# A two-layer hybrid backbone on one core: layer 0's FFN input product by one level of Strassen's algorithm

## The chip, the cores and the metric

The kernel runs on one core of a Trainium2 chip. The time is the device time of one execution in microseconds (us); lower is better. The time before is the median of three runs. The engines are named as in the profile: PE is TensorE (matrix products, with PEld its weight loads), DVE is VectorE, ACT is ScalarE, POOL is GpSimd, SP is the engine whose queue issues the DMAs.

## The reference

Two layers are computed over 512 latent tokens and 256 context tokens with 1024 channels. Each layer normalises its input, multiplies by one combined input projection, runs four mixers (attention, Fourier, convolution, pooling), multiplies their concatenation by `w_out`, adds the residual, and then runs a gated FFN. Layer 1 computes only the latent tokens after its keys and values. What the change touches is the FFN:

```python
def swiglu(x, w_in, w_out):              # D_MODEL 1024, D_FF 2816
    a, g = jnp.split(x @ w_in, 2, axis=-1)
    return (jax.nn.silu(a) * g) @ w_out

    x = x + gate1 * mix
    xn = rms_norm(x, g2) * (1 + scale2) + shift2
    return x + gate2 * swiglu(xn, w_fi, w_fo)
```

In layer 0 this is done for both streams, 768 tokens with the same weights; in layer 1 for the 512 latent tokens.

## The kernel before

Activations lie with channels on the partitions: eight tiles of 128 channels, `x[0]` to `x[7]`, 768 tokens wide. To keep fp32 accuracy with TensorE's rounded fp32 format, each operand is cut into a rounded part (an ACT cast, "h") and the rest (a difference, "l"), and `mm3` makes three matmuls of each product: h x h, h x l, l x h.

A FIFO list `queue` (lines 229 to 260) holds every weight load in the order of use; `need` (line 274) issues up to two entries ahead. A load is one DMA of 512 KB from SP's queue into a raw tile, an ACT cast and a difference of 1024 columns (`split`, line 180) on VectorE or, in the mixers, on POOL (`lo_eng`). All these tiles come from the pool `wp` of 15 buffers, three per load.

The FFN (line 1083) goes over 22 chunks of 128 hidden columns. For a chunk, `ag` (line 1133) makes two products, a and g, each over eight channel tiles: for the 512 latent tokens 48 matmuls of 512 columns, for the 256 context tokens 48 of 256. `glu` (line 1089) then makes silu(a) x g and cuts it into h and l. A step takes two chunks; `out_step` (line 1145) multiplies the two chunks of the step before with `w_ffn_out`: for each of eight output tiles six matmuls of 512 and six of 256 columns, and one VectorE instruction per stream that adds the result to x. In layer 0 a filler makes 1/8 of layer 1's modulation in each step. In the last step the order is: both products of chunk 20, the latent product of chunk 21, the output product of step 9, the latent half of step 10 with the norm of the next layer, and only then the context product of chunk 21 and the context half of step 10. The first step is `first_step` (line 1103), with the channel tiles as the outer loop, since they become ready one after the other: the second norm's `rstd` and `apply` run on VectorE and ACT beside the last `w_out` products (`proj`).

PSUM has eight banks: two tiles `pb` of two banks, two `pt` and two `pf`. The hidden tiles hh and hl rotate over four tags (g, c, u, b). The mixers take their activations from `alp` (16 tiles of 512 columns, latent) and `acp` (16 of 256, context), and have tiles of their own for u, the attention result and the transposed queries.

The framework gives a tile its buffer and each engine its order of instructions when the program is built: it plays the program through a timing model, and at each engine starts the ready instruction that stands earliest in the program. So latent, context and output matmuls are interleaved. On the chip each engine runs its queue in that fixed order.

Of the kernel before, what the change touches and what calls it, by code (L numbers as in the profile page):

```python
# [44 lines left out]
Pace = namedtuple("Pace", "cols taps0 step0 taps side fill share side_n")  # L45
PACE = (Pace(12, 6, 3, 2, 4, 3.0, 0.7, 10), Pace(8, 10, 2, 2, 2, 3.0, 0.3, 8))
# [3 lines left out]
def kernel(ctx: ExitStack, tc: tile.TileContext, xT, ctxT, vec, cst, dft,  # L50
# [16 lines left out]
    tags.update(g0=(816, 1), g1=(816, 1), c0=(784, 1), c1=(784, 1), a0=(768, 1), a1=(784, 1), u0=(768, 1), u1=(768, 1),  # L67
                b0=(792, 1), b1=(792, 1), pr=(784, 3), t=(792, 4), qt=(512, 3))
# [5 lines left out]
    def AL(name, dt=F32R):  # L74
        return alp.tile([P, NL], dt, tag="al", name=name)
# [73 lines left out]
    rtab = [cp.tile([P, 4, HD], F32, name=f"rt{i}") for i in range(4)]  # L149
# [28 lines left out]
    lo_eng = [dve]  # L178
# [49 lines left out]

    for l in range(DEPTH):
        wi = w_in[l]  # L230
        for kp in range(4):
            queue.append((("qkv", l, kp), lambda wi=wi, kp=kp: load(rows(wi[256 * kp:256 * kp + 256, 0:OFF_F]), "wq")))
        for b in range(2):
            for h in range(2):
                queue.append((("c", l, b, h), lambda wi=wi, b=b, h=h: load_conv(wi, b, h)))
        for b in range(2):
            queue.append((("p", l, b), lambda wi=wi, b=b: load(rows(wi[:, OFF_P + 128 * b:OFF_P + 128 * b + 128]), "wi")))
        for h in range(2):
            queue.append((("u", l, h), lambda wi=wi, h=h: load(rows(wi[512 * h:512 * h + 512, OFF_F:OFF_C]), "wi")))
        queue.append((("sm", l), lambda l=l: load_small(l)))  # L240
        queue.append((("dft", l), lambda l=l: load_dft(l)))
        queue.append((("fold", l), lambda l=l: load_fold(l)))
        for m in range(KD):
            queue.append((("o", l, m), lambda l=l, m=m: load(rows(w_out[l][:, 128 * m:128 * m + 128]), "wo")))

        def fa(c, l=l):
            queue.append((("fa", l, c), lambda: load(rows(w_ffn_in[l][:, 128 * c:128 * c + 128]), "fa")))
            queue.append((("fg", l, c), lambda: load(rows(w_ffn_in[l][:, DFF + 128 * c:DFF + 128 * c + 128]), "fg")))

        def fo(c, l=l):  # L250
            queue.append((("fo", l, c), lambda: load(rows(w_ffn_out[l][128 * c:128 * c + 128, :]), "fo")))

        for s in range(NF // 2):
            fa(2 * s)
            if s:
                fo(2 * s - 2)
                fo(2 * s - 1)
            fa(2 * s + 1)
        fo(NF - 2)
        fo(NF - 1)  # L260
# [104 lines left out]
    class Norm:  # L365


        def __init__(self, nm, direct=KD - 2):
            self.direct = direct
            if direct:  # L370
                self.acc = [U(f"acc{nm}{i}", f"a{i}") for i in range(2)]
# [59 lines left out]

    class Acts:


        def __init__(self, nm, ctx_=True):
            self.lt = [[AL(f"{nm}{i}{k}") for k in range(KD)] for i in "hl"]
            self.ct = [[acp.tile([P, NC], F32R, tag="ac", name=f"{nm}c{i}{k}") for k in range(KD)] for i in "hl"] if ctx_ else None

        def at(self, i, k, sl):
            if sl.start >= NL:  # L440
                return self.ct[i][k][:, sl.start - NL:sl.stop - NL]
            return self.lt[i][k][:, sl]
# [6 lines left out]


    def rope_tables(l):
        for i, (off, f) in enumerate(((V_QG, 1.0), (V_KG, HD ** -0.5))):
# [42 lines left out]
    def mix_phase(l, norm, A, filler):  # L495
# [32 lines left out]
        ksb = U("ksb", "a0")  # L528
# [146 lines left out]
        usb = [U(f"us{j}", f"u{j}") for j in range(2)]  # L675
# [86 lines left out]
        def fourier_prep():  # L762
            B, B2 = AL("fb", F32), AL("fd", F32)
# [7 lines left out]
            if not last:  # L771
                C = AL("fc", F32)
# [6 lines left out]
        def fourier():  # L779
# [11 lines left out]
            for b in range(2):  # L791
# [5 lines left out]
                gh, gl = (U(f"g{b}{i}", "ub"[b] + str(i), F32R)[:, 0:768] for i in range(2))  # L797
# [9 lines left out]
            for o in range(2):  # L807
# [5 lines left out]
                q, t = AL("fqs", F32), AL("ft", F32)  # L813
# [13 lines left out]
            for b in range(2):  # L827
# [3 lines left out]
                gh, gl = (U(f"g{b}{i}", "ub"[b] + str(i), F32R)[:, 0:512] for i in range(2))  # L831
# [20 lines left out]
        at = [U(f"at{j}", ("a0", "x5")[j]) for j in range(2)]  # L852
# [4 lines left out]
        def make_qT(i):  # L857
            j, o = qpos(i)
            st = U("qst", "qt", F32R)
# [7 lines left out]
            qTs[i] = U("qT", "qt", F32R)  # L867
            act.copy(out=qTs[i][:, 0:512], in_=ps)
# [167 lines left out]
        def add(m, sl, s, ps):  # L1036
            dve.scalar_tensor_tensor(out=x[m][:, sl], in0=ps, scalar=modT[l][:, 16 + m, s:s + 1], in1=x[m][:, sl],
                                     op0=ALU.mult, op1=ALU.add)
            n2.square(m, sl)

        def proj(m, w, sl, s, ps):
            ps = ps[:, 0:sl.stop - sl.start]
            part(m, w, sl, ps)
            add(m, sl, s, ps)
        first, second = ((HA, 0), (HB, 0)) if last else ((LAT, 0), (CTX, 1))
# [5 lines left out]
        pb1 = None if last else PB("wo2")  # L1051
        for m in range(4):
            w = held[m] = need(("o", l, m))
            part(m, w, LAT, pts[m], order[:6])
        pcs = [] if last else [pb1[:, 0:256], pb1[:, 512:768]]
        for m, pc in enumerate(pcs):
            part(m, held[m], CTX, pc, order[:6])
        for m in range(4):
            part(m, held[m], LAT, pts[m], order[6:])
            add(m, LAT, 0, pts[m])  # L1060
            if m < len(pcs):
                part(m, held[m], CTX, pcs[m], order[6:])
                add(m, CTX, 1, pcs[m])
            elif not last:
                proj(m, held[m], CTX, 1, PF("wo"))
            held.pop(m)
        ahead[0] = 2
        for m in range(4, KD):
            w = held[m] = need(("o", l, m))
            proj(m, w, *first, PA("wo"))  # L1070
        n2.rstd(first[0])
        A = Acts("xf", not last)
        for m in range(2, KD + 2, 2):
            for k in (m - 2, m - 1):
                n2.apply(l, 1, k, *first, A)
            proj(m // 2 + 3, held.pop(m // 2 + 3), *second, PA("wo"))
        n2.rstd(second[0])
# [5 lines left out]
    def ffn(l, norm, first, second, A, filler):  # L1083
# [15 lines left out]
        def newh(c):  # L1099
            tg = ("g", "c", "u", "b")[c % 4]  # L1100
            h[c] = (U("hh", tg + "0", F32R), U("hl", tg + "1", F32R))

        def first_step():
# [3 lines left out]
            for sl, s in (first, second):  # L1107
                n = sl.stop - sl.start
                wide = n == 512
                if wide or last and sl is first[0]:  # L1110
# [52 lines left out]
        first_step()  # L1163
        for s in range(1, ns):
# [136 lines left out]
```

## Time and profile before

| | |
|---|---|
| median of 3 runs | 1496.5 us (1494.83 to 1497.45) |
| profiled execution | 1496.42 us |
| its span, first to last instruction | 1494.6 us |
| instructions | 20629 |
| busy: TensorE, weight loads | 1450.2 us (97%), 1207.1 us (81%) |
| busy: VectorE, ScalarE, POOL | 778.7 us (52%), 541.4 us (36%), 198.3 us (13%) |
| mean granted TensorE clock | 0.993 |

Busy time is the sum of instructions' durations, overlaps counted once. Matmuls overlap, so a full share says that one was always in flight, and not at which rate they came; the rate is read from starts. The granted clock is a share of 2.4 GHz; 0.50 is its lower level of 1.2 GHz.

### The profile page before, as it was taken

To read this page: it belongs to the slowest core of one execution; us is meant where nothing else is said; L and a number is where in the kernel's file an instruction comes from. 1 tells how busy PE (TensorE), PEld (TensorE's weight loads), DVE (VectorE), ACT (ScalarE), POOL (GpSimd) and SP (SyncE) were. 2 spreads that over 40 slices of the span, in tenths; PEclk is the share of its full clock that TensorE was granted. 3 is DMA by queue.
4 is the path that set the end of the run, shared out by engine and by line. 5 is a ranking of instruction groups with operands and counts; after the bars stand their busy time and mean duration, and the time that the engine had idled before them with its cause. 6 is when DMAs were issued, how large, how long until landed. Compare 5 with 4: busy or idle time off the path is not lost.

```text
span 1494.6 us, 20629 instructions
## 1 busy us (share of the span) xinstructions
PE 1450.2 (97%) x8538; PEld 1207.1 (81%) x8538; DVE 778.7 (52%) x1204; ACT 541.4 (36%) x876; POOL 198.3 (13%) x161
## 2 busy tenths in 40 slices
PE   7999889999999999999999999899999999999998
PEld 4687777888888888888888887677789888888887
DVE  3569478354543444344334357587646545444444
ACT  4457656433222112211211234657545322222220
POOL 2435411500000000000000024341330000000000
PEclk9999999999999999999999999999999999999999
DMA  8624444212123213222331231446632323333331
GB/s 281 188 85 149 148 154 131 85 57 83 60 71 99 85 57 99 85 63 79 107 91 43 71 99 57 134 137 198 198 99 87 108 88 99 94 104 90 95 99 57
DMA packets 192926, 157.35 MB, mean 105 GB/s; under 512 B 6464, under 2 KB 179520, under 8 KB 192832
## 3 DMA queue, kind: packets, MB, share of 16 engines
q1 hardware_dynamic: 192544, 155.34, 33.9%
q8 instruction: 67, 1.10, 0.3%
q10 hardware_dynamic: 288, 0.69, 0.1%
q14 instruction: 27, 0.22, 0.0%
HBM read 151.81 MB, written 4.19 MB: 104 GB/s over the span
## 4 chain that ended last, share of the span: by engine, by line
PE 85%; DVE 7%; ACT 3%; DMA 2%; POOL 1%; issue 1%; SPq 0%; DVEq 0%; ACTq 0%
PE ag L161 33%; PE fo L161 21%; PE agc L161 7%; PE wo L161 6%; PE mod L161 3%; PE qkv L161 2%; DVE run L565 2%; PE u L161 2%; PE ssq L161 2%; PE cv L161 1%; PE S L161 1%; PE pv L161 1%; DMA wi<-in_w_in_dram 1%; PE PT L167 1%; PE pp L161 1%
## 5 line engine op out<-in xcount | busy, mean ns | idle before, releaser
L1152 DVE SCALAR_TENSOR_TENSOR x<-fo,mod,x 128x512 f32<-128x512 f32 (+1 forms) x264 | 172.3, 660 | 139.8 <-PE fo L161 139.4
L161 PE MATMUL fo<-hh,foh 128*128 128x512 f32 (+1 forms) x528 | 188.7, 358 | 1.9 <-DVE ht L1095 1.9
L161 PE MATMUL fo<-hh,fol 128*128 128x512 f32 (+1 forms) x528 | 188.8, 357 | 0.0
L161 PE MATMUL fo<-hl,foh 128*128 128x512 f32 (+1 forms) x528 | 188.6, 357 | 0.0
L182 ACT CAST foh<-fo 128x1024 fp32r<-128x1024 f32 x44 | 46.1, 1048 | 275.3 <-PE fo L161 218.5
L161 PE MATMUL ag<-xfh,fah 128*128 128x512 f32 (+1 forms) x368 | 140.4, 386 | 1.2 <-ACT xfh L428 1.2
L161 PE MATMUL ag<-xfl,fah 128*128 128x512 f32 (+1 forms) x368 | 140.7, 382 | 0.6 <-DVE xfl L429 0.5
L161 PE MATMUL ag<-xfh,fal 128*128 128x512 f32 (+1 forms) x368 | 140.5, 382 | 0.0
L161 PE MATMUL ag<-xfh,fgh 128*128 128x512 f32 (+1 forms) x368 | 140.0, 381 | 0.0
L161 PE MATMUL ag<-xfh,fgl 128*128 128x512 f32 (+1 forms) x368 | 140.0, 381 | 0.0
L161 PE MATMUL ag<-xfl,fgh 128*128 128x512 f32 (+1 forms) x368 | 139.8, 380 | 0.0
L161 PEld LDWEIGHTS fo<-hh,foh 128*128 128x128 f32 x528 | 99.6, 189 | 18.9 <-DVE ht L1095 2.1
L161 PEld LDWEIGHTS fo<-hl,foh 128*128 128x128 f32 x528 | 100.0, 189 | 16.7
L161 PEld LDWEIGHTS fo<-hh,fol 128*128 128x128 f32 x528 | 100.1, 190 | 15.7
L105 DVE TENSOR_TENSOR fal<-fa,fah 128x1024 fp32r<-128x1024 f32 x42 | 51.7, 1231 | 101.4 <-ACT fah L182 101.4
L105 DVE TENSOR_TENSOR fgl<-fg,fgh 128x1024 fp32r<-128x1024 f32 x42 | 51.4, 1224 | 97.3 <-ACT fgh L182 86.4
L565 DVE SCALAR_TENSOR_TENSOR run<-glu,vt,run 128x512 f32<-128x512 f32 (+1 forms) x98 | 86.9, 887 | 1.1
L182 ACT CAST fah<-fa 128x1024 fp32r<-128x1024 f32 x44 | 46.2, 1049 | 100.8 <-DMA fa<-in_w_ffn_in_dram 90.2
L182 ACT CAST fgh<-fg 128x1024 fp32r<-128x1024 f32 x44 | 46.1, 1048 | 97.9 <-DMA fg<-in_w_ffn_in_dram 89.1
L161 PEld LDWEIGHTS ag<-xfh,fah 128*128 128x128 f32 x368 | 69.0, 188 | 15.0 <-ACT xfh L428 1.4
L161 PEld LDWEIGHTS ag<-xfl,fah 128*128 128x128 f32 x368 | 69.2, 188 | 14.2 <-DVE xfl L429 1.4
L161 PEld LDWEIGHTS ag<-xfh,fgl 128*128 128x128 f32 x368 | 69.2, 188 | 13.1
(335 smaller groups left out, 3140.8 us busy)
## 6 DMA issues: line engine op xcount, KB each, us to landing
wm<-in_w_mod_dram SPq DMA_DIRECT2D x64, 512.0 KB, 4.6
fa<-in_w_ffn_in_dram SPq DMA_DIRECT2D x44, 512.0 KB, 3.9
fg<-in_w_ffn_in_dram SPq DMA_DIRECT2D x44, 512.0 KB, 3.9
fo<-in_w_ffn_out_dram SPq DMA_DIRECT2D x44, 512.0 KB, 3.3
wm<-in_w_mod_dram SPq DMA_DIRECT2D x40, 256.0 KB, 5.7
wo<-in_w_out_dram SPq DMA_DIRECT2D x16, 512.0 KB, 5.3
wm<-in_w_mod_dram SPq DMA_DIRECT2D x16, 384.0 KB, 5.6
x<-in_xT_dram SPq DMA_DIRECT2D x16, 256.0 KB, 4.1
```

Source lines behind the costliest of these rows:

```text
L105: eng.tensor_tensor(out=out, in0=full, in1=b32(hi), op=ALU.subtract)
L161: i = last_pe[0] = pe.matmul(*a, **kw)
L167: i = last_pe[0] = pe.transpose(*a)
L182: act.copy(out=hi[:, :n], in_=raw[:, :n])
L565: yield dve.scalar_tensor_tensor(out=cacc[b][:, :cwid] if j == CONVW - 1 else run, in0=glu[b][:, j:j + cwid], scalar=tap(b, j), in1=cacc[b ...
L1152: dve.scalar_tensor_tensor(out=x[m][:, sl], in0=ps[:, :n], scalar=modT[l][:, 40 + m, st:st + 1], in1=x[m][:, sl], op0=ALU.mult, op1=ALU.add)
```

## The change

Layer 0 (`FAST = (True, False)`) keeps the ordinary product for chunks 0 and 1. For chunks 2 to 21 the product of the 256 x 1024 weight block (a on top of g) with the 1024 x 768 activations is split in two along each of its three dimensions: output rows a and g, channels 0 to 511 and 512 to 1023, tokens 0 to 383 and 384 to 767. Winograd's form of Strassen's algorithm makes it with 7 products of half size, four sums of weights and four of activations, and seven additions of results. Each product has four channel tiles and three matmuls of 384 columns. The sums are made in fp32, and then cut into h and l: weights seven times 512 columns per chunk (all on VectorE and ACT), activations once for the layer. `w_out` of layer 0 is made in two halves of 384 tokens too, the second with one instruction more where the streams meet. In the last step chunk 21's product is made before the output products, and both halves of the latent stream come before the context stream.

To make room, tiles of 768 columns in one pool of 28 (`alp`) hold the operands, the mixers' activations of both streams, u, the first attention result, the queries, the rotary tables and one norm sum; Fourier scratch tiles move into `wp`, which goes from 15 to 14 buffers; and hidden tiles rotate over three tags. The scratch for DMA descriptors is set to 1024. Both layers' mixers use the shared pool.

```diff
-    alp = ctx.enter_context(tc.tile_pool(name="alp", bufs=16))
-    acp = ctx.enter_context(tc.tile_pool(name="acp", bufs=16))
-    wp = ctx.enter_context(tc.tile_pool(name="wp", bufs=15))
+    alp = ctx.enter_context(tc.tile_pool(name="alp", bufs=28))
+    wp = ctx.enter_context(tc.tile_pool(name="wp", bufs=14))
...
+    def load_ff(l, c):
+        raws = []
+        for o in (0, DFF):
+            raw = RAW("ff")
+            nc.sync.dma_start(out=raw.rearrange("p (a b) -> p a b", b=P), in_=rows(w_ffn_in[l][:, o + P * c:o + P * c + P]))
+            raws.append(raw)
+        a1, a2, g1, g2 = (r[:, 512 * i:512 * i + 512] for r in raws for i in range(2))
+        ops = {}
+        def cut(nm, full):
+            w = ops[nm] = W("f" + nm)
+            hi, lo = w[:, 0:512], w[:, 512:1024]
+            act.copy(out=hi, in_=full)
+            sub_lo(lo_eng[0], lo, full, hi)
+        def comb(out, in0, in1, op):
+            sum_eng[0].tensor_tensor(out=out, in0=in0, in1=in1, op=op)
+        cut("a11", a1)
+        cut("a12", a2)
+        cut("a22", g2)
+        comb(g2, g1, g2, ALU.add)
+        comb(g1, a1, g1, ALU.subtract)
+        comb(a1, g2, a1, ALU.subtract)
+        comb(a2, a2, a1, ALU.subtract)
+        for nm, full in (("s2", a1), ("s3", g1), ("s1", g2), ("s4", a2)):
+            cut(nm, full)
+        return ops
...
+    class Operands:
...
+        def cut(self, nm, k, full, eng=None):
+            act.copy(out=self.h(nm, k), in_=full)
+            sub_lo(eng or dve, self.l(nm, k), full, self.h(nm, k))
...
+        def second(self, norm, l, half):
+            n = self.n
+            for k in range(4):
+                f = self.f1[k] = AL("bf", F32)
+                norm.full(l, 1, k, half, f[:, 0:n])
+                self.cut("b12", k, f[:, 0:n])
+            for k in range(4):
+                b12, b22 = self.f1[k][:, 0:n], self.f1[k][:, n:2 * n]
+                b11, b21 = self.f2[k][:, 0:n], self.f2[k][:, n:2 * n]
+                norm.full(l, 1, 4 + k, half, b22)
+                self.cut("b22", k, b22)
+                for out, in0, in1 in ((b11, b12, b11), (b12, b22, b12), (b22, b22, b11), (b21, b21, b22)):
+                    tsum_eng[0].tensor_tensor(out=out, in0=in0, in1=in1, op=ALU.subtract)
...
         def newh(c):
-            tg = ("g", "c", "u", "b")[c % 4]
+            if FAST[l] and c == NF - 1:
+                h[c] = (AL("hh"), AL("hl"))
+                return
+            tg = ("g", "c", "b")[c % 3]
...
+        def fast(c, ops):
+            n = A.n
+            banks = []
+            def product(w, b):
+                if not banks:
+                    pb = PB("ag")
+                    banks.extend((pb[:, 0:n], pb[:, 512:512 + n]))
+                out = banks.pop(0)
+                for k in range(4):
+                    mm3(out, ops[w][:, P * k:P * k + P], ops[w][:, 512 + P * k:512 + P * k + P], A.h(b, k), A.l(b, k), k == 0, k == 3)
+                return out
...
+            act.copy(out=cu[:, lo_], in_=product("a11", "b11"))
+            add(s_[:, lo_], product("a12", "b21"), cu[:, lo_])
+            add(cu[:, hi_], product("s2", "t2"), cu[:, lo_])
+            add(y_[:, lo_], product("s3", "t3"), cu[:, hi_])
+            p5 = product("s1", "t1")
+            add(g_[:, hi_], p5, y_[:, lo_])
+            add(y_[:, hi_], p5, cu[:, hi_])
+            add(g_[:, lo_], product("a22", "t4"), y_[:, lo_])
+            close(lo_)
+            banks[:] = [PA("agl")[:, 0:n]]
+            add(s_[:, hi_], product("s4", "b22"), y_[:, hi_])
+            close(hi_)
...
+        def fast_steps():
+            fast_first()
+            for s in range(1, ns):
+                fin = s == ns - 1
+                newh(2 * s)
+                fast(2 * s, need(("ff", l, 2 * s)))
+                if fin:
+                    newh(2 * s + 1)
+                    fast(2 * s + 1, need(("ff", l, 2 * s + 1)))
+                wo = [need(("fo", l, 2 * s - 2)), need(("fo", l, 2 * s - 1))]
...
+                else:
+                    for sl, st in streams:
+                        out_step(s - 1, sl, st, wo, False)
+                    newh(2 * s + 1)
+                    fast(2 * s + 1, need(("ff", l, 2 * s + 1)))
```

`add` is one VectorE addition of 384 columns with one operand in PSUM. `close` makes, for one token half, silu (ACT), the product with g (VectorE), the cast (ACT) and the difference (VectorE). `fast_first` makes chunks 0 and 1 for the two token halves in turn, with `second` between them, and after them the 16 cuts of the activation sums t1 to t4.

## Rows read from the trace of the kernel before

**Rows 1.** The page, part 1: busy time and share of each engine.
```profile
PE 1450.2 (97%) x8538; PEld 1207.1 (81%) x8538; DVE 778.7 (52%) x1204; ACT 541.4 (36%) x876; POOL 198.3 (13%) x161
```

**Rows 2.** The page, part 4: the chain that ended last, by engine.
```profile
PE 85%; DVE 7%; ACT 3%; DMA 2%; POOL 1%; issue 1%; SPq 0%; DVEq 0%; ACTq 0%
```

**Rows 3.** Windows: length, busy PE, PEld, DVE, ACT, POOL, clock, DMA, GB/s.
```profile
200.00:250.00 50.00, 44.75 (x358) 33.76 (x359) 47.39 (x98) 33.43 (x85) 2.36 (x1) 0.93 0.35 106
...
320.00:340.00 20.00, 19.55 (x117) 17.21 (x117) 19.44 (x26) 9.91 (x16) 1.08 (x1) 1.00 0.44 133
400.00:850.00 450.00, 450.00 (x2666) 391.77 (x2665) 185.24 (x275) 94.21 (x134) 0.00 (x0) 1.00 0.26 79
894.00:899.00 5.00, 4.63 (x25) 4.61 (x26) 2.75 (x8) 3.12 (x6) 2.54 (x2) 0.66 0.09 26
```

**Rows 4.** Timeline of ScalarE: start, duration, instruction; the first and last.
```profile
465.41 0.37 ACT L323 COPY me<-mod 128x256 f32<-128x256 f32 x1 [0.18 <-PE mod L161]
...
774.84 0.37 ACT L323 COPY me<-mod 128x256 f32<-128x256 f32 x1
```

**Rows 5.** Timeline of TensorE, matmuls of 512 columns, first and last of 33.
```profile
344.44 0.39 PE L161 MATMUL ag<-xfh,fgh 128*128 128x512 f32 x1
...
351.70 0.39 PE L161 MATMUL ag<-xfh,fgl 128*128 128x512 f32 x1
```

**Rows 6.** Timeline of TensorE, matmuls of 256 columns, first and last of 79.
```profile
318.14 0.28 PE L161 MATMUL wo<-mxch,wol 128*128 128x256 f32 x1
...
327.49 0.28 PE L161 MATMUL wo<-mxch,wol 128*128 128x256 f32 x1
```

**Rows 7.** VectorE's groups, 400 to 850 us: busy us, mean ns, idle before.
```profile
L1152 DVE SCALAR_TENSOR_TENSOR x<-fo,mod,x 128x512 f32<-128x512 f32 x64 | 47.9, 750 | 45.4 <-PE fo L161 45.4
L1152 DVE SCALAR_TENSOR_TENSOR x<-fo,mod,x 128x256 f32<-128x256 f32 x68 | 32.9, 484 | 44.4 <-PE fo L161 44.4
L105 DVE TENSOR_TENSOR fol<-fo,foh 128x1024 fp32r<-128x1024 f32 x19 | 23.3, 1226 | 6.4 <-ACT foh L182 6.0
L105 DVE TENSOR_TENSOR fal<-fa,fah 128x1024 fp32r<-128x1024 f32 x17 | 20.8, 1226 | 51.4 <-ACT fah L182 51.4
...
L105 DVE TENSOR_TENSOR hl<-ht,hh 128x512 fp32r<-128x512 f32 x18 | 12.5, 693 | 12.4 <-ACT hh L1096 12.4
L1095 DVE TENSOR_TENSOR ht<-ht,ag 128x512 f32<-128x512 f32 x18 | 12.3, 683 | 51.7 <-ACT ht L1094 51.7
L105 DVE TENSOR_TENSOR hl<-ht,hh 128x256 fp32r<-128x256 f32 x18 | 7.6, 421 | 2.8 <-ACT hh L1096 2.8
L1095 DVE TENSOR_TENSOR ht<-ht,agc 128x256 f32<-128x256 f32 x18 | 7.5, 417 | 10.5 <-ACT ht L1094 10.5
```

**Rows 8.** Timeline of VectorE: instructions that follow one another without idle time.
```profile
353.39 0.69 DVE L105 TENSOR_TENSOR hl<-ht,hh 128x512 fp32r<-128x512 f32 x1
353.99 0.48 DVE L429 SCALAR_TENSOR_TENSOR xfcl<-xt,mod,xfch 128x256 fp32r<-128x256 f32 x1
354.39 0.48 DVE L426 SCALAR_TENSOR_TENSOR xt<-x,a,R 128x256 f32<-128x256 f32 x1
```

**Rows 9.** ScalarE's groups, 400 to 850 us, columns as in rows 7.
```profile
L182 ACT CAST foh<-fo 128x1024 fp32r<-128x1024 f32 x19 | 19.9, 1049 | 179.7 <-PE fo L161 166.6 <-DMA fo<-in_w_ffn_out_dram 12.4 <-PE agc L161 0.7
...
L1096 ACT CAST hh<-ht 128x512 fp32r<-128x512 f32 x18 | 11.2, 621 | 18.3 <-DVE ht L1095 18.3
```

**Rows 10.** Timeline of TensorE at the end of layer 0's FFN.
```profile
894.37 0.39 PE L161 MATMUL fo<-hh,foh 128*128 128x256 f32 x1 [1.89 <-DVE ht L1095]
...
898.17 0.30 PE L161 MATMUL fo<-hh,foh 128*128 128x256 f32 x1
```

**Rows 11.** Timeline of POOL, the first two of layer 0's w_out pieces.
```profile
206.33 2.36 POOL L105 TENSOR_TENSOR wol<-wo,woh 128x1024 fp32r<-128x1024 f32 x1 [6.83 <-ACT woh L182]
253.99 2.38 POOL L105 TENSOR_TENSOR wol<-wo,woh 128x1024 fp32r<-128x1024 f32 x1 [45.30 <-ACT woh L182]
```

**Rows 12.** The page, part 6: DMA issues, KB each, median us to landing.
```profile
fa<-in_w_ffn_in_dram SPq DMA_DIRECT2D x44, 512.0 KB, 3.9
```

More of the change, by code (lines that the diff above doesn't have):

```diff
@@ L148 @@
     aT = [cp.tile([P, 2, KD, 2], F32, name=f"a{l}") for l in range(DEPTH)]
[L149 removed]
+    rtab = [None] * 4
     gsw = [cp.tile([P, 4, HD], F32, name="gs")] * DEPTH
@@ L430, in apply, with full @@
                                      op0=ALU.add, op1=ALU.subtract)
+        def full(self, l, i, k, pieces, dst):
+            o, R = pieces[0][0].start, self.R[pieces[0][0].start]
+            n = pieces[-1][0].stop - o
+            t = U("xt", "t")
+            for sl, s in pieces:
+                c = slice(sl.start - o, sl.stop - o)
+                dve.scalar_tensor_tensor(out=t[:, c], in0=x[k][:, sl], scalar=aT[l][:, i, k, s:s + 1],
+                                         in1=R[:, c], op0=ALU.mult, op1=ALU.mult)
+            for sl, s in pieces:
+                c = slice(sl.start - o, sl.stop - o)
+                act.activation(out=dst[:, c], in_=t[:, c], func=AF.Identity, bias=modT[l][:, 24 * i + k, s:s + 1])
     class Acts:
@@ L674, in mix_phase @@
             next(cols, None)
-        usb = [U(f"us{j}", f"u{j}") for j in range(2)]
+        usb = [AL(f"us{j}", F32) for j in range(2)]
         def u_at(i):
@@ L850, in fourier @@
                 yield 1.3
-        at = [U(f"at{j}", ("a0", "x5")[j]) for j in range(2)]
+        at = [U("at1", "x5") if j else AL("at0", F32) for j in range(2)]
         qTs = {}
@@ L1034, in part, with adds, whole, proj @@
                 mm3(ps, w[0][:, P * k:P * k + P], w[1][:, P * k:P * k + P], M.h(k, sl), M.l(k, sl), k == order[0], k == order[-1])
[L1036 to L1045, printed above, removed]
+        def adds(m, half, ps):
+            for sl, s in half:
+                dve.scalar_tensor_tensor(out=x[m][:, sl], in0=ps[:, sl.start - half[0][0].start:sl.stop - half[0][0].start],
+                                         scalar=modT[l][:, 16 + m, s:s + 1], in1=x[m][:, sl], op0=ALU.mult, op1=ALU.add)
+            n2.square(m, whole(half))
+        def whole(half):
+            return slice(half[0][0].start, half[-1][0].stop)
+        def proj(m, w, half, ps):
+            ps = ps[:, 0:whole(half).stop - whole(half).start]
+            part(m, w, whole(half), ps)
+            adds(m, half, ps)
+        if last:
+            first, second = [(HA, 0)], [(HB, 0)]
+        elif FAST[l]:
+            first, second = [(slice(0, 384), 0)], [(slice(384, 512), 0), (CTX, 1)]
+        else:
+            first, second = [(LAT, 0)], [(CTX, 1)]
         held = {}
@@ L1069, in mix_phase @@
             w = held[m] = need(("o", l, m))
-            proj(m, w, *first, PA("wo"))
-        n2.rstd(first[0])
-        A = Acts("xf", not last)
+            proj(m, w, first, PA("wo"))
+        n2.rstd(whole(first))
+        A = Operands(whole(first).stop) if FAST[l] else Acts("xf", not last)
         for m in range(2, KD + 2, 2):
             for k in (m - 2, m - 1):
-                n2.apply(l, 1, k, *first, A)
-            proj(m // 2 + 3, held.pop(m // 2 + 3), *second, PA("wo"))
-        n2.rstd(second[0])
+                if FAST[l]:
+                    A.first(n2, l, k, first)
+                else:
+                    n2.apply(l, 1, k, *first[0], A)
+            proj(m // 2 + 3, held.pop(m // 2 + 3), second, PA("wo"))
+        n2.rstd(whole(second))
         for _ in filler:
@@ L1106, in first_step @@
                 newh(c)
-            for sl, s in (first, second):
+            for sl, s in first + second:
                 n = sl.stop - sl.start
                 wide = n == 512
-                if wide or last and sl is first[0]:
+                if wide or last and sl is first[0][0]:
                     pbs = [PB("ag") for _ in range(2)]
@@ L1162, in ffn @@
         ns = NF // 2
-        first_step()
-        for s in range(1, ns):
+        if FAST[l]:
+            fast_steps()
+        else:
+            first_step()
+        for s in range(1, 1 if FAST[l] else ns):
             fin = s == ns - 1
```

139 lines of the change are left out of this document (110 added, 29 removed).

## The prediction

> **What bounds the kernel now.** I read the busy shares first: TensorE shows 1450.2 of 1494.6 us, 97% [rows 1]. A busy TensorE alone proves little, so next comes the chain of work that ended last: 85% of it is TensorE [rows 2]. Then the windows, because the change lies in one stage: from 400 to 850 us, the FFN of layer 0, TensorE is busy all 450 us at a granted clock of 1.00 (the 2.4 GHz level), while VectorE is busy 185.24 us, 41% [rows 3]. In that stretch nothing releases TensorE late; it is bound by its own instructions. The repeating unit is a step of two column chunks. Its period is read from the ScalarE copy that comes once a step: the first and the last of seven successive ones stand at 465.41 and 774.84 us, so 309.43 / 6 = 51.57 us a step [rows 4].
>
> How long a matmul holds TensorE is not the duration in a row, for they overlap; it is the distance from start to start. Rows of 512 columns: 32 distances between 344.44 and 351.70 us, 0.227 us each [rows 5]. Rows of 256: 78 distances between 318.14 and 327.49 us, 0.120 us each [rows 6]. The line through both has a slope of 0.107 / 256 = 0.417 ns a column and a fixed part of 0.013 us. A chunk's input product has 48 matmuls of each width: 48 x 0.347 = 16.65 us.
>
> **The change, part by part.** The profiled execution took 1496.42 us, 1.8 more than its span, and the median of the three timed runs is 1496.5; the sum is made against 1496.4.
>
> *Matmuls.* For chunks 2 to 21 (chunks 0 and 1 keep the ordinary product, in two halves of 384 tokens) there are 7 products of 4 x 3 matmuls of 384 columns, 84 in place of 96. No row has 384 columns. From below, per-column pricing of the 512 row: 0.75 x 0.227 = 0.170 us; from above, one and a half 256 rows: 0.180 us. I take the line, 0.1734, exactly the middle of the two widths. A chunk is then 84 x 0.1734 = 14.57 us and saves 2.08 us; 20 chunks save 41.6 us. The ends give 47.2 (at 0.170, 14.28 us a chunk) and 30.6 us (at 0.180, 15.11 us). Chunks 0 and 1, w_out and its norm sums only split 512 + 256 columns into 384 + 384: nothing by the same line.
>
> The Trainium skill, page "TensorE: Matmul & The Clock Gate", section "Back-to-back issue gap", prices a warm matmul at N / 2.4 + 2.5 ns. The rows above lie some 11 ns higher at both widths. By the page a chunk would go from 15.6 to 13.65 us and 20 chunks would save 39.0 us; that is an estimate from the page, and the sum keeps 41.6.
>
> *VectorE, the cover of everything that is added.* Added per chunk: seven cuts of 512 columns (a ScalarE cast and a VectorE difference each) for two of 1024, four weight combinations of 512, seven additions out of PSUM of 384 columns, and the gate's product and difference in two halves. Prices: 512-wide SBUF difference 0.693 us, the combination likewise; PSUM operand 0.683 (512) and 0.417 (256), so 0.55 at 384; SBUF at 384 between 0.693 and 0.421, so 0.56 [rows 7]. Per step of two chunks: 22 x 0.693 = 15.2; 14 x 0.55 = 7.7; 8 x 0.56 = 4.5; unchanged the residual additions 8 x (0.750 + 0.484) = 9.9 and two differences of 1024, 2.5. Together 39.8 us, where 41% of 51.57, 21.1, stood before. The new step is 51.57 - 2 x 2.08 = 47.4 us, so VectorE is filled to 84%: still hidden, with 7.6 us to spare. The recorded durations overstate it, though: a 512-wide difference begins at 353.39 and the next instruction at 353.99, 0.60 us later for 0.69 recorded; 256-wide ones follow at 0.40 us for 0.48 [rows 8]. Some 0.09 less for each of 62 instructions is 5.6 us, and the fill 34.2 / 47.4 = 72%. That TensorE can run beside a full VectorE is seen from 320 to 340 us: 19.44 of 20 us VectorE, 19.55 TensorE [rows 3].
>
> [...]
>
> ScalarE gains seven casts of 512 a chunk at 0.621 us in place of two of 1024 at 1.049 [rows 9], and five passes of 384 for four of 512 and 256. At some 0.5 us the five take 2.5 us, so that is 6.9 us a chunk: far below 47 us a step.
>
> *Waits in a chunk.* Products fill PSUM in pairs of banks, two pairs in turn. The fifth product needs the first pair back; products three and four (2 x 2.08 = 4.2 us) cover its two evacuations. Behind a late addition in VectorE's queue stand the other additions of the chunk and the weight cuts of the next; TensorE waits for them. Bounds for that: 0 (TensorE is busy throughout the present stage) to the 1.89 us that the one hurried gate of this layer costs today [rows 10], in each chunk, 38 us. I take 0.3 a chunk, nearer to the stage's own rows, 6 us.
>
> *Weight buffers in the stage.* A step claims 2 x 9 + 2 x 3 = 24 of 14 buffers, where it claimed 18 of 15. A buffer is thus claimed anew some 14 / 24 x 47.4 = 28 us after its last claim, 43 us before. In that time a chunk's two transfers (3.9 us each [rows 12]) and its eleven VectorE instructions (7.6 us) fit, while SP's queue holds the loads of w_ffn_out behind a late one. Zero while it fits; if it does not, it shows as the wait just priced.
>
> *The head.* The second half's operands (24 differences x 0.56, and eight normalisations at 0.75 or a little over, as they come in two pieces: some 20 us of VectorE) lie beside chunk 0 and 1's first half, 192 matmuls x 0.1734 = 33 us. The T cuts lie beside the second. Between 0 and 5 us; I take 1.
>
> *The tail of the stage.* Now the last 256-column product is followed by its gate in a hurry: TensorE waits 1.89 us for VectorE, and then its granted clock is 0.66 from 894 to 899 us: 18 matmuls between 894.37 and 898.17 us take 0.211 us each (the 1.2 GHz level, 213 ns for 256 columns) [rows 3, 10]. That costs 18 x (0.211 - 0.120) = 1.6 us more. After the change chunk 21 is complete before either output product, so both go: 0 to 3.5 us gained; I take 2, since the norm's reciprocals fall due in that place as before.
>
> *Layer 1.* Its hidden tiles rotate over three tags, not four: chunk 21 reuses chunk 18's, read by the output product just ahead of its own use. A cast and a difference stand in the open there, up to 0.621 + 0.693 = 1.3 us and the clock; I take 1.
>
> *The mixers.* 28 wide tiles take what 16 + 16 narrower and eight fixed ones held, with some room; but weight buffers go from 15 to 14 and Fourier scratch moves into them. The present kernel already shows that shortage: the second w_out piece's POOL difference comes 45.30 us after the first [rows 11]. In SP's queue a load that waits for a buffer holds all loads behind it. If each of four pieces came late by one cast and difference (1.049 + 2.38 us [rows 9, 11]) in both layers, that is 27 us; below nothing, -5 us, as in the 50 us from 200 on TensorE idles 5.25 us [rows 3] and a new order may win that back. I take 2.
>
> Sum: 1496.4 - 41.6 + 6 + 1 - 2 + 1 + 2 = 1462.8, say 1463 us. The likeliest case's own range is 1453 to 1473.
>
> **Rivals.**
> - *VectorE sets the step: slower.* Its queue is a fixed order. If nothing is placed behind a cut while its ScalarE cast runs, each of 14 cuts costs 0.62 us of VectorE, each of four gate differences 0.69 (12.4 us over 18 [rows 7]), two fo cuts 1.05: 8.7 + 2.8 + 2.1 = 13.6 on 39.8, 53.4 us a step against 51.57. Ten steps: 18 us slower, 1514. It decides from 11.8 us of such waits a step. For it: `fal` waits 51.4 us over 17 for its cast today [rows 7]. Against it: those waits stand where VectorE had nothing to do. The T cuts and combinations offer work to put there.
> - *The mixers take it back: still faster.* As priced above, up to 27 us, with the likeliest other terms 1463 + 20 = 1483. For it: rows 11; against it: the wide pool is larger, and TensorE's own wait for w_out is short.
> - *Everything is hidden.* No waits, all of the tail won: 1496.4 - 41.6 - 3.5 = 1451.
> - *It does not do what it says.* If 384 columns cost what 512 do, a chunk takes 84 x 0.227 = 19.1 us, 2.4 more than now: 1545. The slope of 0.417 ns, one column per cycle of 2.4 GHz, speaks against it.
>
> **Numbers.** Forecast (1453 to 1473) 0.57; everything hidden 0.09; mixers or waits take part of it (1473 to 1493.4) 0.18; within 0.2%, which is about what a measurement of this kernel can tell from no change (1493.4 to 1499.4), 0.03; slower 0.13, nearly all of it VectorE. So faster 0.84. The range 1450 to 1491 leaves out the slower cases and a little on either side.
>
> **What would show it.** Right: TensorE busy throughout the stage, 12 fewer matmuls a chunk, start to start near 0.173 us at 384 columns; a step near 47.4 to 48 us; VectorE at 72 to 84% of it; no wait at the stage's end. Wrong: TensorE rows released by VectorE inside the chunks, or a granted clock under 1.00 there; matmuls of 384 columns nearer 0.2 us; new waits for loads or POOL at the start of either w_out.

## The result and the profile after

The changed kernel takes 1475.3 us (median of 4 runs, 1474.25 to 1476.14) against 1497.0 for the kernel before beside it (1494.83 to 1500.58): ratio 0.9852, interval 0.9832 to 0.9873. It is faster: the interval leaves out 1, though the difference is under 2%. The time lies in the stated range of 1450 to 1491, but 2.3 us outside the likeliest case's own 1453 to 1473: what came is the case "mixers or waits take part of it", which had a chance of 0.18. It is 12 us above the forecast of 1463: of a gain of 33 us, 22 came. The profiled execution took 1474.25 us, with a span of 1472.5.

The page of the kernel after, busy time by engine and the chain that ended last, to set beside [rows 1] and [rows 2]:

```profile
PE 1417.3 (96%) x8298; PEld 1217.2 (83%) x8298; DVE 945.2 (64%) x1572; ACT 600.2 (41%) x1035; POOL 199.3 (14%) x161
...
PE 83%; DVE 7%; ACT 4%; DMA 4%; issue 1%; POOL 1%; SPq 0%; ACTq 0%; DVEq 0%; POOLq 0%
```

The same window as in [rows 3], and the ScalarE copy that comes once a step, as in [rows 4], of the kernel after:

```profile
400.00:850.00 450.00, 448.62 (x2622) 417.96 (x2621) 343.80 (x600) 144.72 (x254) 0.00 (x0) 1.00 0.28 84
```
```profile
565.05 0.37 ACT L360 COPY me<-mod 128x256 f32<-128x256 f32 x1 [3.81 <-PE mod L161]
...
756.15 0.37 ACT L360 COPY me<-mod 128x256 f32<-128x256 f32 x1 [3.72 <-PE mod L161]
```

Two matmuls of 384 columns, the first and the last of twelve in a row in w_out, a width that [rows 5] and [rows 6] do not have:

```profile
263.50 0.33 PE L161 MATMUL wo<-mxh,woh 128*128 128x384 f32 x1
...
265.40 0.33 PE L161 MATMUL wo<-mxh,wol 128*128 128x384 f32 x1
```

The steady stage is as forecast. The two copies are four steps apart: 191.10 / 4 = 47.78 us a step, where 47.4 to 48 was given. Eleven distances in 1.90 us make 0.173 us for 384 columns. VectorE is busy 343.80 of 450 us, 76%, and TensorE 448.62. So the loss lies outside the steps. The starts of the first matmul of each stage cut the span of each kernel's one profiled execution into four stretches (us; the first holds the mixer of layer 0 and w_out, the third those of layer 1). The profiled execution is not always near the median: that of head_early took 1456.72 us, its fastest, that of tail_wql 1466.87, its second slowest.

| kernel | median | ratio to before | to first FFN product | FFN 0 | layer 1 to its FFN | rest |
|---|---|---|---|---|---|---|
| before | 1497.0 | 1 | 327.9 | 576.7 | 218.5 | 371.5 |
| after | 1475.3 | 0.9852 | 336.3 | 545.8 | 218.7 | 371.7 |
| off_pools | 1508.9 | 1.0070 | 336.7 | 579.5 | 221.9 | 370.5 |
| qt_own | 1475.0 | 0.9848 | 331.0 | 546.0 | 226.5 | 371.8 |
| fqs_shared | 1473.8 | 0.9843 | 337.3 | 545.7 | 217.8 | 371.7 |
| qt_fqs | 1462.4 | 0.9758 | 328.8 | 545.5 | 215.6 | 370.8 |
| off_homes | 1497.1 | 1.0000 | 329.4 | 577.7 | 219.4 | 370.5 |
| head_early | 1459.2 | 0.9750 | 324.8 | 540.7 | 218.0 | 371.4 |
| tail_wql | 1462.6 | 0.9783 | 326.6 | 544.5 | 222.6 | 371.4 |
| head_tail | 1459.9 | 0.9761 | 325.9 | 541.3 | 216.5 | 371.8 |
| adds_twice | 1477.4 | 0.9872 | 326.9 | 558.4 | 215.4 | 370.5 |
| tail_order | 1463.0 | 0.9784 | 328.5 | 535.7 | 225.1 | 371.1 |
| tail_wo_order | 1461.4 | 0.9771 | 326.4 | 536.1 | 225.4 | 371.2 |
| tail_both | 1456.1 | 0.9724 | 326.7 | 535.7 | 220.8 | 371.1 |

The first stretch varies by up to 4 us where no edit aimed at it (328.8 us in qt_fqs, 324.8 in head_early). Each edit also makes the framework plan every engine's order anew, which the third stretch shows most.

Kernel after against before: 8.4 us lost ahead of the first FFN product, 30.9 gained in FFN 0 (forecast 36.6), 0.2 and 0.2 lost behind it.

### The profile page after: what moved, and what is told of

The parts are those of the page before. It is cut to its first block, busy times and chain, and to the rows that moved or that the text cites. A ratio compares the mean times of both kernels' runs of the same rounds, so it can differ in the third digit from the quotient of the medians.

```text
span 1472.5 us, 20702 instructions
## 1 busy us (share of the span) xinstructions
PE 1417.3 (96%) x8298; PEld 1217.2 (83%) x8298; DVE 945.2 (64%) x1572; ACT 600.2 (41%) x1035; POOL 199.3 (14%) x161
## 4 chain that ended last, share of the span: by engine, by line
PE 83%; DVE 7%; ACT 4%; DMA 4%; issue 1%; POOL 1%; SPq 0%; ACTq 0%; DVEq 0%; POOLq 0%
PE ag L161 35%; PE fo L161 20%; PE wo L161 6%; PE qkv L161 4%; PE cv L161 3%; PE agl L161 3%; PE mod L161 3%; DVE run L669 3%; PE u L161 2%; PE ssq L161 1%; PE S L161 1%; DMA wm<-in_w_mod_dram 1%; PE pv L161 1%; PE PT L167 1%; PE cc L161 1%
## 5 line engine op out<-in xcount | busy, mean ns | idle before, releaser
L161 PE MATMUL ag<-t,fs 128*128 128x384 f32 x720 | 136.6, 336 | 0.9 <-DVE hg L1266 0.9
L161 PEld LDWEIGHTS ag<-t,fs 128*128 128x128 f32 x720 | 125.0, 188 | 6.4 <-issue 1.6
L161 PE MATMUL ag<-b,fa 128*128 128x384 f32 x480 | 92.6, 336 | 1.5 <-DVE ht L1216 1.5
L105 DVE TENSOR_TENSOR fol<-fo,foh 128x1024 fp32r<-128x1024 f32 x44 | 53.8, 1222 | 54.1 <-ACT foh L182 41.9
L161 PEld LDWEIGHTS ag<-b,fa 128*128 128x128 f32 x480 | 83.4, 188 | 3.4 <-DVE ht L1216 1.8
L161 PE MATMUL wo<-mxh,wol 128*128 128x384 f32 (+2 forms) x224 | 73.7, 330 | 0.0
L161 PE MATMUL wo<-mxl,woh 128*128 128x384 f32 (+2 forms) x224 | 73.5, 329 | 0.0
L161 PE MATMUL wo<-mxh,woh 128*128 128x384 f32 (+2 forms) x224 | 73.5, 331 | 0.1
L161 PE MATMUL ag<-xfh,fah 128*128 128x512 f32 (+1 forms) x192 | 71.3, 376 | 1.2 <-ACT xfh L465 1.2
L161 PE MATMUL ag<-xfl,fah 128*128 128x512 f32 (+1 forms) x192 | 71.6, 373 | 0.8 <-DVE xfl L466 0.8
```

Source lines behind the costliest of these rows:

```text
L105: eng.tensor_tensor(out=out, in0=full, in1=b32(hi), op=ALU.subtract)
L161: i = last_pe[0] = pe.matmul(*a, **kw)
```

## Experiments

### The mixers: two shortages, one behind the other

The timeline of ScalarE near the end of layer 0's attention, kernel before: two of the copies of transposed probabilities (pt), the last cast of a query tile (qst), and the last transposed query tile (qT).

```profile
202.69 0.59 ACT L906 COPY pt<-PT 128x512 f32<-128x512 f32 x1
208.75 0.61 ACT L906 COPY pt<-PT 128x512 f32<-128x512 f32 x1
...
222.49 0.41 ACT L862 CAST qst<-q 128x256 fp32r<-128x256 f32 x1
...
236.27 0.59 ACT L868 CAST qT<-qT 128x512 fp32r<-128x512 f32 x1
```

The same of the kernel after:

```profile
201.38 0.58 ACT L1012 COPY pt<-PT 128x512 f32<-128x512 f32 x1
228.66 0.59 ACT L1012 COPY pt<-PT 128x512 f32<-128x512 f32 x1
...
236.10 0.41 ACT L968 CAST qst<-q 128x256 fp32r<-128x256 f32 x1
...
247.03 0.59 ACT L974 CAST qT<-qT 128x512 fp32r<-128x512 f32 x1 [0.16 <-PE qT L167]
...
251.81 1.28 ACT L1044 ACT_TABLE_LOAD   x1
...
253.82 1.28 ACT L997 ACT_TABLE_LOAD   x1
...
256.69 1.28 ACT L1060 ACT_TABLE_LOAD   x1
```

No probabilities are copied for 27 us, from 201.38 to 228.66, while the Fourier products go through; then attention's last query tiles come late and collide with the convolution's functions on ScalarE (three table loads of 1.28 us). The first w_out product comes at 262.3 us instead of 250.5. Two of the new homes could do that: pt shares the weight pool with the Fourier scratch, and the query tiles share the wide pool with the Fourier operands.

**off_pools**: only the pools and tags of the change. The switch takes out Strassen's products and with them the two halves of w_out and the new order of the last step.

```diff
-FAST = (True, False)
+FAST = (False, False)
```

> Strassen is switched off in both layers; the shared pool, the weight pool of 14 and the moved tags stay. Theory A (the 8.4 us that the first layer's mixer lost come from the new homes of its tiles): the mixer is late by as much as in the changed kernel, its first w_out product at about 262 us instead of 250.5, the first FFN product 8 to 12 us late, and the whole takes 1504 to 1509 us. Rival B (the loss comes with Strassen's own part: the 384-column halves of w_out, the operand loads fetched ahead): the mixer is as early as before and the time is 1495 to 1499 us.

1508.94 us (1507.02 to 1510.4), ratio 1.007 (1.005 to 1.0089): theory A. The first w_out product comes at 261.9 us, the first FFN product at 336.7. The new homes alone make the kernel before 0.7% slower.

**qt_own** and **fqs_shared**: each home by itself.

```diff
-                b0=(792, 1), b1=(792, 1), pr=(784, 3), t=(792, 4))
+                b0=(792, 1), b1=(792, 1), pr=(784, 3), t=(792, 4), qt=(512, 2))
...
-            st = AL("qst")
+            st = U("qst", "qt", F32R)
...
-            qTs[i] = AL("qT")
+            qTs[i] = U("qT", "qt", F32R)
```
```diff
-                qt = W("fqs", F32)
-                q, t = qt[:, 0:512], qt[:, 512:1024]
+                q, t = AL("fqs", F32), AL("ft", F32)
```

> The query tiles (qst, qT) get two buffers of their own again, out of the shared pool; room for them comes from narrower scratch columns and from the rope tables' gain tile. Theory A1 (the last query tiles wait for a shared buffer that the Fourier operands hold): the first w_out product comes at about 251 to 255 us and the time is 1467 to 1471 us. Theory A2 (attention's transposed probabilities, pt, wait for weight-pool buffers that the Fourier scratch holds): the same as the changed kernel, 1474 to 1477 us.

> Only the Fourier scratch fqs goes back from the weight pool to the shared pool, as two tiles as before the change. Theory A2: the probabilities find buffers, the first w_out product comes at 251 to 255 us, 1467 to 1471 us. Theory A1: nothing changes, 1474 to 1477 us.

> Both together. Theory A, by either of its parts or by both: the first layer's attention is interleaved with the Fourier products as before, one table load fewer stands in it, the first w_out product comes at 249 to 252 us, and the time is 1464 to 1468 us. Rival B: 1474 to 1477 us.

qt_own: 1475.04 us (1473.93 to 1477.11); the first w_out product comes at 255.2 us, as A1 has it, and the first stretch is 5.3 us shorter, but layer 1's mixer takes 7.8 us longer. The traces say where: in that stretch TensorE's waits come to 17.3 us instead of 13.7, and the missing clock (time x (1 - granted clock), summed over pieces of 5 us) to 7.7 instead of 3.4. What made the new order wait there was not studied. fqs_shared: 1473.77 us (1473.1 to 1477.59), no gain in the first stretch. By their totals A1 and A2 both fall; in the first stretch A1 is right in part. **qt_fqs**, both edits together: 1462.4 us (1457.62 to 1465.07), ratio 0.9758 (0.9734 to 0.9783), 12.9 us less than the kernel after. The same view shows why moving the scratch alone does nothing. First fqs_shared, then qt_fqs:

```profile
214.33 0.59 ACT L1011 COPY pt<-PT 128x512 f32<-128x512 f32 x1 [0.45 <-PE mod L161]
...
231.67 0.41 ACT L967 CAST qst<-q 128x256 fp32r<-128x256 f32 x1
```
```profile
214.25 0.59 ACT L1012 COPY pt<-PT 128x512 f32<-128x512 f32 x1 [0.86 <-PE mod L161]
...
220.22 0.41 ACT L968 CAST qst<-q 128x256 fp32r<-128x256 f32 x1
...
233.26 0.59 ACT L974 CAST qT<-qT 128x512 fp32r<-128x512 f32 x1 [0.27 <-PE qT L167]
```

With the scratch moved, pt goes on at 214.33, and attention then stands for its next query tile until 231.67. With both, it stands for neither, and is done before the first convolution table load.

**off_homes**: the homes of qt_fqs, Strassen off.

> Strassen off in both layers, with the homes of the fourth run (query tiles with two buffers of their own, Fourier scratch in the shared pool). Theory A: what the shared pools cost is undone without Strassen as well, the first FFN product comes at 327 to 329 us and the time is 1494 to 1499 us, as before; the products saved are then worth the distance to the fourth run, 32 to 36 us. Rival: the fourth run is faster by a lucky order in the second layer and the pools still cost here, 1502 to 1509 us.

1497.08 us (1494.61 to 1502.06), ratio 1.000 (0.9986 to 1.0014). With these two homes nothing is left of the pools' cost, and what the switch takes out (Strassen's products, their head and tail, the halves of w_out) is worth 1497.1 - 1462.4 = 34.7 us.

### The head of the FFN

The timeline of VectorE in the kernel after, where the second half's operands are made (xt, bf, b):

```profile
345.62 2.55 DVE L451 RECIPROCAL R<-R 128x384 f32<-128x384 f32 x1 [0.64 <-ACT R L450]
356.23 0.56 DVE L1216 TENSOR_TENSOR ht<-ht,ag 128x384 f32<-128x384 f32 x1 [8.06 <-ACT ht L1215]
356.70 1.40 DVE L476 SCALAR_TENSOR_TENSOR xt<-x,a,R 128x128 f32<-128x128 f32 x4
```

The norm is ready at 348.2, the gate (ht, silu times g) is what VectorE waits for, and the operands stand behind it. The gate comes with the last of the first half's 96 products, of which these rows hold the first two and the last:

```profile
336.31 0.81 PE L161 MATMUL ag<-b,fah 128*128 128x384 f32 x2
...
355.04 0.34 PE L161 MATMUL ag<-b,fgl 128*128 128x384 f32 x1
```

TensorE's waits from 336 to 384 us, by what released it (us in total, times, longest), all that there are, and the same in qt_fqs:

```profile
PE ag L161 <- DVE b L105: 1.7, 2, 1.0
PE ag L161 <- DVE ht L1216: 1.5, 1, 1.5
```

**head_early**, on qt_fqs:

```diff
+            A.second(norm, l, second)
             for z in range(2):
...
                     out = [PA("ag")[:, 0:n] for i in range(4)]
-                    A.second(norm, l, second)
```

> On the fourth run: the operands of the second column half are emitted ahead of the first half's products instead of behind them. Theory H: VectorE's 8 us of idle time at the head of the FFN are used, TensorE's waits of 1.46, 0.78 and 0.96 us there shrink to 1.5 us or less in all, and the time is 1458.5 to 1461 us. Rival: the operands wait for something else (a buffer, the norm), or their work now stands in front of the gate's evacuation: 1461.5 to 1465 us.

1459.22 us (1456.72 to 1463.44), ratio 0.975 (0.973 to 0.977). VectorE now goes on at once:

```profile
334.07 2.55 DVE L451 RECIPROCAL R<-R 128x384 f32<-128x384 f32 x1 [0.67 <-ACT R L450]
336.66 3.38 DVE L476 SCALAR_TENSOR_TENSOR xt<-x,a,R 128x128 f32<-128x128 f32 x10
```

The three waits are gone, and FFN 0 takes 540.7 us instead of 545.5. Theory H held in the stage; by the totals alone the two kernels' ranges overlap. The gain of 4.8 us is more than the 3.2 of the waits; two later ones of qt_fqs, 0.73 us near 470 us and 0.77 near 842, went too, 4.7 us in all.

### The tail of the FFN

The end of layer 0's FFN in the kernel after: TensorE, GpSimd, VectorE. ssq sums the squares for layer 1's first norm by a matmul with ones, acca and acda are partial sums on GpSimd and VectorE, and wql is the low part of layer 1's first weights.

```profile
868.56 0.38 PE L161 MATMUL fo<-hh,foh 128*128 128x256 f32 x1 [1.39 <-DVE x L1362]
...
878.46 1.12 PE L161 MATMUL ssq<-acca,ones 128*128 128x256 f32 x2 [3.98 <-POOL acca L437]
```
```profile
874.32 2.35 POOL L105 TENSOR_TENSOR wql<-wq,wqh 128x1024 fp32r<-128x1024 f32 x1 [2.60 <-DMA wc<-in_w_in_dram]
876.62 0.92 POOL L437 TENSOR_TENSOR acca<-acca,sq 128x256 f32<-128x256 f32 x1
```
```profile
864.85 3.35 DVE L451 RECIPROCAL R<-R 128x512 f32<-128x512 f32 x1
...
874.89 2.06 DVE L437 TENSOR_TENSOR acda<-acda,sq 128x256 f32<-128x256 f32 x1 [0.60 <-ACT sq L436]
876.87 0.47 DVE L1362 SCALAR_TENSOR_TENSOR x<-fo,mod,x 128x256 f32<-128x256 f32 x1
877.27 0.55 DVE L437 TENSOR_TENSOR acda<-acda,sq 128x256 f32<-128x256 f32 x1
```

So there are two waits: 1.39 us for x, whose additions stand behind a reciprocal of 3.35 us, and 3.98 us for the last squares' sum. The experiments go after the second; the first is still 1.40 us in the fastest version.

**tail_wql** (on qt_fqs) and **head_tail** (on head_early, the sums too):

```diff
-        lo_eng[0] = pool
+        lo_eng[0] = dve if l else pool
...
         ahead[0] = 2
+        lo_eng[0] = pool
         rope_tables(l)
```

> On the fourth run: the low parts of layer 1's first four weight tiles (wql) are made by VectorE instead of GpSimd. Theory T: at the end of the FFN the squares' sum on GpSimd no longer stands behind 2.35 us of wql, the sum on VectorE beside it takes 0.55 us instead of 2.05, TensorE's wait of 3.7 us before the last ssq shrinks to 1.5 to 2.2 us, and the time is 1459.5 to 1461.5 us. Rival: VectorE has no room there and is late itself: 1462 to 1465 us.

> On the fourth run: both of these, and the squares' sums of the norm after the FFN all on VectorE. Theories H and T: the gains add up, 1455.5 to 1459.5 us. Rivals: one of them or none, 1460 to 1464 us.

tail_wql: 1462.57 us (1461.29 to 1469.86), no gain. The wait fell only from 3.7 to 3.0 us, and in its profiled execution, 4.3 us above its median, layer 1 took 7.0 us longer. head_tail: 1459.87 us (1457.29 to 1466.18), what head_early gives alone; its wait is 3.9 us. Theory T falls: with wql out of the way, ScalarE's cast of the next weights still waits for its DMA in front of the squares. ScalarE in head_tail:

```profile
859.96 1.04 ACT L182 CAST wch<-wc 128x1024 fp32r<-128x1024 f32 x1 [3.53 <-DMA wc<-in_w_in_dram]
```

**tail_order**: those casts behind the squares (`behind` fixes an order of two instructions on one engine; `mark` is the last square).

```diff
-        act.copy(out=hi[:, :n], in_=raw[:, :n])
+        i = act.copy(out=hi[:, :n], in_=raw[:, :n])
+        if after[0] is not None:
+            behind(i, after[0])
...
+            after[0] = mark[0] if k[0] in ("qkv", "c") and k[1] == 1 else None
             ready[k] = f()
+            after[0] = None
```

> On the head_early run: in ScalarE's order the casts of layer 1's weights that its FFN fetched late (two wqh, four wch) stand behind the squares of the last norm instead of between them; nothing else is changed. Theory T2 (the wait at the FFN's end comes from a cast that waits for its DMA in front of the squares): TensorE's wait before the last ssq falls from 4.1 to 1 to 2 us and the first qkv product comes 2 to 3 us earlier behind the first FFN product, 538 to 539 us instead of 540.7. Rival: the casts are then late for the qkv products, which wait as long; 540 to 542 us. In all 1455 to 1460 us, by what the second layer's order makes of it.

1462.98 us (1462.2 to 1465.96), so not faster than head_early (1456.72 to 1463.44), and theory T2's total fails, though it held where it was aimed: the first wait is 1.25 us instead of 4.10, and FFN 0 takes 535.7 us, 5.0 less. The norm's matmuls behind the shorter wait also keep the granted clock of 1.00 (861 to 866 us), where head_early has 0.71 behind its wait (860 to 865 us). The gain is lost again a few products later. TensorE, VectorE and GpSimd at the start of layer 1:

```profile
862.38 0.70 PE L161 MATMUL ssq<-acca,ones 128*128 128x256 f32 x2 [1.25 <-POOL acca L443]
...
869.21 0.50 PE L161 MATMUL qkv<-wqh,xnl 128*128 128x512 f32 x1 [3.69 <-DVE xnl L472]
```
```profile
863.86 0.16 DVE L347 TENSOR_REDUCE mod<-mods 128x4 f32<-128x16 f32 x1
864.05 2.15 DVE L348 TENSOR_TENSOR mod<-mod,vt 128x4 f32<-128x4 f32 x1
866.24 2.26 DVE L328 SCALAR_TENSOR_TENSOR a<-mod,vt 128x4 f32<-128x4 f32 x1
868.42 1.40 DVE L472 SCALAR_TENSOR_TENSOR xnl<-xt,mod,xnh 128x512 fp32r<-128x512 f32 x2
```
```profile
863.52 4.96 POOL L105 TENSOR_TENSOR wql<-wq,wqh 128x1024 fp32r<-128x1024 f32 x2 [1.19 <-ACT wqh L182]
```

The two instructions of four columns end at 866.20 and 868.50 us, GpSimd's two wql at 866.18 and 868.48, and the operand xnl stands behind them.

**tail_both**: tail_order and the edit of tail_wql.

> As tail_order, and the low parts of layer 1's weights that its first products need (wql, wcl) are made by VectorE instead of GpSimd. Theory C (in tail_order VectorE's four-column instructions at the start of layer 1 took 2.15 and 2.26 us instead of 0.15 because GpSimd made wql beside them, and TensorE waited 3.69 us for what stood behind): they take 0.2 us again, TensorE's wait there falls below 1.5 us, the first qkv product still comes 535 to 537 us behind the first FFN product, and the time is 1453 to 1458 us. Rival: the six casts' low parts, 1.2 us each, now delay VectorE by as much; 1459 to 1464 us.

1456.11 us (1455.25 to 1458.42), ratio 0.9724 (0.9705 to 0.9743). Theory C held; TensorE's 3.69 us became 0.41, in VectorE's timeline the two are:

```profile
863.26 0.15 DVE L348 TENSOR_TENSOR mod<-mod,vt 128x4 f32<-128x4 f32 x1
...
864.66 0.15 DVE L328 SCALAR_TENSOR_TENSOR a<-mod,vt 128x4 f32<-128x4 f32 x1
```

It is the fastest version, 2.8% under the kernel before, but its interval overlaps head_early's.

### Layer 1's w_out

**tail_wo_order**, as tail_order, and from w_out's fifth tile on `after` is the square root of the convolution's norm.

> As tail_order, and in layer 1 the casts of w_out's fifth and later tiles stand behind the layer norm's square root in ScalarE's order. Theory T3 (the table load and the root of layer 1's convolution norm wait behind a cast that waits for its DMA, TensorE then stands 2.3 us and runs the next 8 us at half clock): from the first w_out product to the first FFN product of layer 1 54 to 56.5 us instead of 59.4, and the time is 1451 to 1456 us. Rival: w_out's products wait for the later casts instead: 58 to 61 us, 1456 to 1460 us.

1461.35 us (1459.84 to 1465.16), and 59.5 us from w_out to FFN: theory T3 falls. The wait of 2.4 us for the root shrank to 1.1, but the casts then stood in front of csh (the convolution's input to its product, in rounded form), for which TensorE waited 3.8 us instead of 1.8.

### VectorE's cover

**adds_twice**, on qt_fqs:

```diff
             def add(out, ps, other):
-                dve.tensor_tensor(out=out, in0=ps, in1=other, op=ALU.add)
+                for _ in range(2):
+                    dve.tensor_tensor(out=out, in0=ps, in1=other, op=ALU.add)
```

> On the fourth run (qt_fqs): each of the seven sums that VectorE makes from PSUM in a Strassen chunk is made twice, 7 x 0.55 us more a chunk, 7.7 us more a step; the second one writes what the first wrote. Theory (TensorE sets the step, VectorE has the cover that its 72 to 84% say): a step stays between 47.7 and 49.5 us, TensorE's waits in the chunks stay below 2 us a step, and the time is 1462 to 1480 us. Rival (VectorE is close to setting the step, because each sum also holds a PSUM bank that the next product needs): a step of over 50 us, 1485 us or more.

1477.43 us (1473.01 to 1479.98). TensorE's waits from 400 to 850 us, by what released it:

```profile
PE ag L161 <- DVE hy L1267: 4.2, 2, 3.8
PE ag L161 <- DVE hg L1267: 2.6, 5, 1.0
PE agl L161 <- DVE fs L105: 0.7, 1, 0.7
```

FFN 0 takes 558.4 us, in qt_fqs 545.5: 1.3 us for each of ten steps for 7.7 us more of VectorE's work, which fills it to 88% (306.86 of 350 us from 450 on) instead of 76%. 3.8 us of the waits is one at the stage's end. The theory held: VectorE does not set the step, and there was room for most of this.

## Why the prediction was right, and where its sizes were off

The mechanism is the one forecast: TensorE is the limit, it has 240 matmuls fewer, and VectorE's new work stays hidden. What was off are terms around it, nearly all to the same side.

- **Matmuls, -41.6: right.** 240 matmuls fewer, 0.173 us at 384 columns. Once the head and the tail are mended FFN 0 takes 535.7 instead of 576.7 us, 41.0 less, with waits of TensorE in it of 2.6 and 2.8 us. (The term's upper end is 47.4 by its own factors, not 47.2.)
- **Waits in the chunks, +6: a little high, and near by luck.** The step fell by 51.57 - 47.78 = 3.79 us where 4.16 is the price of the matmuls: 3.7 us over ten steps. But TensorE's waits from 400 to 850 us come to 1.4 us, of which 0.9 were for an addition of VectorE, the mechanism that was priced; the rest lies in distances between matmuls that the profile does not call waits. VectorE at 76% lies between the two fills given. The rival in which VectorE sets the step, and with it the slower side, is refuted at 7.7 us more a step.
- **The mixers, +2: the term that failed most.** Measured are 8.4 us in layer 0 and 0.2 in layer 1. The prediction named the shortage of weight buffers [rows 11] and priced late w_out pieces; the runs show that what waits for a buffer is attention: pt for the weight pool, and behind it the query tiles for the wide pool, of which I had written that it has some room. The bound of 27 us held it. (With that bound in place of the 2 the sum gives 1488; the 1483 of the rival is 5 us low.)
- **Head, +1, and tail, -2: mis-sized.** FFN 0 gained 30.9 us where ten steps give 37.9, so together they cost 7.0; TensorE's waits in the whole of FFN 0 went from 2.8 to 9.9 us. The head rests on a wrong count: some 20 us of operands were laid beside 33 us of products, 192 matmuls, but those are both halves. The first half has 96, which took from 336.31 to 355.04 us. And of that time VectorE stood idle for 8.06 us, since the operands stand in its queue behind a gate that comes with the last of those products. In the tail the gate's wait of 1.89 us [rows 10] went as foreseen, and the reciprocal that was named cost 1.39 us. What was not foreseen is that the squares of the norm come late, 3.98 us: they stand behind the next layer's casts, and GpSimd's sum behind the wql made from one of them, as tail_order shows. In the order before, the context product of chunk 21 stands between the two output products; that it gave the casts their time there is likely, but no run tests it alone. The sign "no wait at the stage's end" did not come.
- **Layer 1's hidden tiles, +1: nothing.** 0.2 us.

The misses add to 6.6 (mixers) + 5.7 (the FFN: 36.6 - 30.9) - 0.8 = 11.5 us; forecast and measured gain of the span are 33.6 and 22.1.

The 11 us by which layer 1's mixer moves between the kernels are TensorE's waits and the clock behind them. In that stretch its waits are 9.5 us (qt_fqs) to 17.3 (qt_own), the missing clock, summed as above, is 3.4 to 8.5 us, and what is left is 199.5 to 202.4 us in all fourteen. In head_early, for one, TensorE stands 2.3 and 1.9 us in w_out, and its granted clock is 0.66 from 1044 to 1054 us. Open is why the framework's new order makes more of these waits in one kernel than in another, in qt_own for one.

## What to carry to other kernels

A buffer taken from one tag for another was paid here in the mixers, far from the change: list who draws on the pool at each point. Two shortages in series hide each other: moving the scratch alone gained nothing, giving the query tiles their buffers alone 5.3 us of the stretch and nothing in the total, and both together 12.9 us. In a fixed queue, ask of each new instruction what it stands behind; "it fits beside" is a statement on sums, and says nothing of order, and the sum itself wants a count of what really stands there. And a wait that is mended gives its time to the next in the chain: measure a stage by its own starts as well as by the total.

## What the runs showed of the hardware

Small VectorE instructions that read two operands from SBUF became as long as what GpSimd had in hand: 0.15 us for 128 x 4 became 2.15 and 2.26 in tail_order and was 0.15 again when GpSimd's wql was gone; the sum of 256 columns took 2.06 in the kernel after and 0.55 two instructions later. A reduction of 128 x 16 from PSUM beside the same wql kept its 0.16 us. The other way round a wcl of GpSimd, else 2.40 us, took 9.27 in qt_fqs beside a row of VectorE instructions without a gap; the row ended at 891.79 us, the wcl 2.3 us later. GpSimd, and the last VectorE instructions beside it:

```profile
884.79 9.27 POOL L105 TENSOR_TENSOR wcl<-wc,wch 128x1024 fp32r<-128x1024 f32 x1 [7.78 <-PE qkv L161]
```
```profile
890.25 1.54 DVE L463 SCALAR_TENSOR_TENSOR xt<-x,a,R 128x512 f32<-128x512 f32 x3
```

The Trainium skill, page "SBUF — State Buffer", section "Who interferes with whom", says that a VectorE instruction with two inputs in SBUF contends with a GpSimd instruction that reads SBUF, and that the ports they share are an exclusive lock; these rows agree.

In head_early the granted clock fell after the two waits of 2.3 and 1.9 us in w_out, to 0.57 from 1049 to 1054 us. In TensorE's timeline the convolution's product then has 0.43 us from start to start for 512 columns. In qt_fqs, with the second wait alone, the clock stayed at 1.00 and the same product took 0.23. First head_early, then qt_fqs:

```profile
1050.03 0.63 PE L161 MATMUL pw<-csh,sml 128*128 128x512 f32 x1
1050.45 0.63 PE L161 MATMUL pw<-csh,smh 128*128 128x512 f32 x1
```
```profile
1057.29 0.40 PE L161 MATMUL pw<-csh,smh 128*128 128x512 f32 x1
1057.52 0.39 PE L161 MATMUL pw<-csl,smh 128*128 128x512 f32 x1
```
